# Conditioning the first half of the channels first, and row and column groups for the samples' small products

## The chip, the core and the metric

The kernel runs on one core of one Trainium2 chip. The metric is the device time of one execution in microseconds (us), less is better. The engines are TensorE (PE, the matmuls; its weight loads are shown apart as PEld), VectorE (DVE), ScalarE (ACT), GpSimd (POOL) and SyncE (SP, which issues most of the transfers). Each engine works through its own instructions in the order of the program, and waits at the head of that row for what its next instruction needs.

## The reference, cut to what matters

One layer for 1024 prompt tokens and 8 requests of 8 sample tokens (64 columns more, 1088 in all), 1024 channels, fp32:

```
mod = silu(c) @ w_ada + b_ada
sh1, sc1, g1, sh2, sc2, g2 = split(mod, 6)          # 1024 each
h = rms_norm(x, norm_mix_pre) * (1 + sc1) + sh1
proj = h @ w_in                                     # z, xbc, dt, qkv, gate, beta, alpha
# SSD: 16 heads x 64, state (64, 128) per head;  GDN: 8 heads, state (128, 128) per head
# for a sample request b (8 tokens) the state that comes in is state_ssd[b], state_gdn[b]:
y_off  = C @ h_in * exp(acs)                        # SSD: product with the old state
h_last = h_in * exp(acs_end) + B^T @ (x dt decay)   # SSD: the state's update
v_new  = U - W @ S ;  o = q_in @ S + attn @ v_new   # GDN: products with the old state
S_last = S * g_end + k_out^T @ v_new                # GDN: the state's update
x = x + g1 * rms_norm(concat(y, o) @ w_out)
x = x + g2 * rms_norm(swiglu(modulated rms_norm(x)))
```

The prompt's requests start from a state of zeros, the samples' 8 requests each from a state of their own. All new states are outputs.

## The kernel before

**Large products.** A weight tile is split in a high part (`wh`, cast on ACT, L161) and the rest (`wl`, subtracted on DVE, L162), the activations likewise (`hh`, `hl`), and a product is three matmuls (L186 to L188 in `gemm`, L1262 to L1265 for w_out). The 1088 columns go in thirds, `TH` = 384, 384 and 320. Of the weights, `load_tile` brings 128 columns in two halves of 0.26 MB.

**Order.** PE's row of instructions is that in which the code is written (`manual_schedule` of PE); the scheduler orders the other engines. Smaller work is written as generators, started with `spawn`. `gemm` calls `tick()` after k = 2, 5 and 7, and each tick lets every generator go on to its next `yield`. So the SSD pairs (`ssd_pair`) and the samples' GDN (`gdn_samples`) stand between the large products, as does `hidden_rest`, which makes the second and third thirds of the hidden columns.

**The beginning.** `ada_block(cb)` loads 512 columns of w_ada (2 MB) and multiplies (L255): the 1024 rows are taken 128 at a time, and k modulo 4 picks 32 of the PE's columns, so four products go to four groups of 32 output partitions. `ada_cols` folds the four groups and turns the result into channels on partitions (L281), into `modT` (shift: blocks 0 and 1; scale: blocks 2 and 3). The blocks come in the order 0, 1, 2, 3, with the loads of x tiles 0 to 2 between them on SP, then come the weights of K and Q and x3 to x8. `norm_x` (ACT L246, DVE L118 and L248) scales x rows, `turned` transposes (L307), and `modulated` gives `hh` (ACT L338), `ht` (DVE L340) and `hl` (DVE or POOL L349). For the first third all eight k are made, and then the gemms of K and Q run.

**SSD samples.** A pair of heads handles 128 state rows. For each half a (4 requests) the old state is transposed to `h0T` (a tile `hS`, three buffers, ACT copy L1047), and 4 matmuls of 128x128 weights with 8 columns each give the product with C (L1063). At the end L1077 is the last use of the decay tile `L`, of which there are two, and then the state is updated in two matmuls with 64 rows of weights and 512 columns (L1084, one per half, with a yield between). `decays` (L976 to L983) makes the next pair's `L`: a load, nine subtractions on DVE per head, an exponential on ACT; L995 multiplies it by `cb`, and L1044 uses it.

**GDN samples.** Per head and request one matmul of 128x128 weights and 128 columns, eight summed in one bank (L1436): the weights `kb` hold the request's k and q in 8 columns of its own each and zeros elsewhere. L1444, L1454 follow, then the update in two matmuls of 64 rows and 512 columns (L1461), with a yield behind each.

Of the kernel before, what the change touches and what calls it, by code (L numbers as in the profile page):

```python
# [8 lines left out]
F32 = mybir.dt.float32  # L9
# [7 lines left out]
P = 128  # L17
D = 1024
KD = D // P
NP = 1024  # L20
# [23 lines left out]
def hybrid_step(ctx: ExitStack, tc: tile.TileContext, x_p, x_s, c_p, c_s, st_ssd, st_ssdc, st_gdn, st_gdnc,  # L44
# [60 lines left out]
    sel = const.tile([P, 9], F32, name="sel")  # L105
    dve.tensor_tensor(out=sel, in0=fold[:, 0:9], in1=ident[:, 9:10].to_broadcast([P, 9]), op=ALU.add)
# [111 lines left out]
    cc = gk.tile([P, NP], F32, name="gate")[0:9]  # L218
    act.dma_start(out=cc[0:1, :], in_=c_p)
    act.dma_start(out=cc[1:9, :], in_=c_s)  # L220
    act.activation(out=cc, in_=cc, func=AF.Silu)
    pool.memset(caF, 0.0)
    ps = bank()
    pcv = ps[:, 0:KD * 9].rearrange("p (k n) -> p k n", n=9)
    for k in range(KD):
        pe.transpose(pcv[:, k, :], cc[:, k * P:(k + 1) * P], ident[0:9, 0:9])
    dve.tensor_copy(caF[:, :, 0:9], pcv)
# [7 lines left out]
    def load_x(i):  # L235
# [4 lines left out]
        sp.dma_start(out=xt[0:n], in_=x_p[i * P:(i + 1) * P, :] if i < NC else x_s)  # L240
# [8 lines left out]


# [6 lines left out]
    bias = [init.tile([P, 512], F32, name=f"bias{i}") for i in range(2)]  # L257
    for t in bias:
        pool.memset(t, 0.0)

    def ada_block(cb, between):
        ps = ps_a.tile([P, 512], F32, name="ps")
        act.dma_start(out=bias[cb % 2][9:10, :], in_=b_ada[:, cb * 512:(cb + 1) * 512])
        for k in range(0, KD, 2):
# [4 lines left out]
            if k == 2:  # L269
                between()  # L270
            if cb == 3 and k == 4:
                turn.extend(turned(0, i) for i in range(2))
        rows = init.tile([P, 512], F32, name="rows", bufs=2)
        dve.tensor_tensor(out=rows, in0=ps, in1=bias[cb % 2], op=ALU.add)
        return rows

    def ada_cols(cb, rows):
        ps = bank()
        pv = ps[:, 0:4 * 9].rearrange("p (k n) -> p k n", n=9)
        for i in range(4):  # L280
            pe.matmul(pv[:, i, :], lhsT=rows[:, i * P:(i + 1) * P], rhs=sel, start=True, stop=True)  # L281
        dve.tensor_copy(modT[:, cb // 2, 4 * (cb % 2):4 * (cb % 2) + 4, :], pv)
# [4 lines left out]
    act.dma_start(out=r1[0:8, :], in_=n_mix_pre[0].rearrange("(r c) -> r c", c=P))  # L287
    act.dma_start(out=r1[8:16, :], in_=n_ffn_pre[0].rearrange("(r c) -> r c", c=P))
    act.dma_start(out=r1[16:24, :], in_=ssd_nw[0].rearrange("(r c) -> r c", c=P))
    act.dma_start(out=r1[24:25, :], in_=gdn_nw)  # L290
    act.dma_start(out=r1[25:37, :], in_=ssd_cb[0].rearrange("(r c) -> r c", c=P))
    act.dma_start(out=r1[37:85, :], in_=ssd_cw[0].rearrange("j (r c) -> (j r) c", c=P))
    act.dma_start(out=r2, in_=gdn_cw[0].rearrange("j (r c) -> (j r) c", c=P))
    def params():
        ps = bank()
# [14 lines left out]
    turn = []  # L310
    rows = ada_block(0, params)
# [5 lines left out]
    for i in (3, 4, 5):  # L317
        load_x(i)
    first.append(load_tile(w_in, C_Q))
    for i in (6, 7, 8):  # L320
        load_x(i)
    ada_cols(3, rows)
    W_MIX, W_FFN, W_SSDN, W_GDNN = (prm1T[:, a:b] for a, b in ((0, 8), (8, 16), (16, 24), (24, 25)))
# [10 lines left out]
    def modulated(ps, k, c0, n, hi, lo, pool_, low=dve):  # L334
# [7 lines left out]
        if m < n:  # L342
# [8 lines left out]
    dve.scalar_tensor_tensor(out=modT[:, 1], in0=modT[:, 1], scalar=1.0,  # L351
                             in1=W_MIX.unsqueeze(2).to_broadcast([P, KD, 9]), op0=ALU.add, op1=ALU.mult)

    hid_box = {}

    def hidden(g, step):
        c0, n = TH[g]
        for k in range(KD):
# [32 lines left out]
    for _ in hidden(0, KD):  # L391
        pass
# [1441 lines left out]
```

## Time and profile before

| | us |
|---|---|
| median of 3 runs | 2081.65 (2078.68 to 2083.41) |
| the profiled execution | 2084.96 |
| its span in the profile | 2083.2 |
| PE busy | 2003.6 (96%) |
| DVE busy | 1380.3 (66%) |
| ACT busy | 940.1 (45%) |
| POOL busy | 240.9 (12%) |

A row of a timeline gives the start, the time that the instruction took, the engine, the line, the operation with output and inputs, the tile's rows and columns for PE, and how many instructions of the same kind follow one another. Behind them in brackets stands how long the engine was idle before, and what ended that. Starts on PE are measured and ends modelled, so distances are taken from start to start. A plain fp32 matmul shows as two records (x8 are four matmuls).

### The profile page before, as it was taken

The page shows a single profiled execution, that of the slowest core. Times are in us where ns is not written, and L with a number is a line of the kernel's source. Part 1 is how long each engine was busy: PE and PEld are TensorE (multiplying, and loading weights), DVE is VectorE, ACT ScalarE, POOL GpSimd, SP SyncE. Part 2 cuts the span into 40 slices and gives each one's busy share as a digit, 9 for nine tenths or more (in the row PEclk, how much of TensorE's full clock was granted, in tenths as well). Part 3 has the DMA queues.
Part 4 walks back from the last instruction along what each step waited for, and adds up shares of the span by engine and source line. Part 5 has one row for each costly group of instructions (what it writes and reads, how often), then busy time and mean ns, then how long its engine had stood idle before and what let it go on. Part 6 is the DMA issues. An engine that isn't in the chain of part 4 may idle for free. (4 is left out here: it accounts for less than half of the span.)

```text
span 2083.2 us, 35078 instructions
## 1 busy us (share of the span) xinstructions
PE 2003.6 (96%) x13075; PEld 1783.9 (86%) x13075; DVE 1380.3 (66%) x3071; ACT 940.1 (45%) x2241; POOL 240.9 (12%) x238
## 2 busy tenths in 40 slices
PE   6999999999999999899999999999999999999998
PEld 3888999999999988788867667899999999988886
DVE  3769787788778548657647758895555556745465
ACT  3545545554544443334423447663333334544354
POOL 2211010011100023323213210000000000000000
PEclk9999999999999999999999999999999999999999
DMA  9122121121111266465466757532222223643131
GB/s 295 29 69 55 38 63 52 51 64 50 53 56 57 75 203 196 141 207 185 151 214 199 233 157 223 153 91 78 78 79 78 79 73 107 226 141 107 46 100 48
DMA packets 224763, 239.45 MB, mean 115 GB/s; under 512 B 19141, under 2 KB 177391, under 8 KB 224464
## 3 DMA queue, kind: packets, MB, share of 16 engines
q1 hardware_dynamic: 218320, 232.33, 36.0%
q10 hardware_dynamic: 5952, 3.75, 0.6%
q8 instruction: 103, 1.69, 0.3%
q0 software_dynamic: 320, 1.12, 0.2%
q14 instruction: 68, 0.56, 0.1%
HBM read 190.92 MB, written 46.25 MB: 114 GB/s over the span
## 5 line engine op out<-in xcount | busy, mean ns | idle before, releaser
L186 PE MATMUL ps<-hh,wh 128*128 128x384 f32 (+1 forms) x1248 | 445.4, 357 | 1.5 <-ACT sz L566 1.5
L187 PE MATMUL ps<-hl,wh 128*128 128x384 f32 (+1 forms) x1248 | 412.4, 330 | 2.8 <-DVE hl L349 1.6
L188 PE MATMUL ps<-hh,wl 128*128 128x384 f32 (+1 forms) x1248 | 411.2, 329 | 0.0
L1262 PE MATMUL ps<-wh,sh 128*128 128x512 f32 x678 | 277.7, 410 | 3.3 <-ACT wh L161 2.5
L1265 PE MATMUL ps<-wl,sh 128*128 128x512 f32 x678 | 270.8, 399 | 3.6 <-DVE wl L162 3.5
L186 PEld LDWEIGHTS ps<-hh,wh 128*128 128x128 f32 x1248 | 238.7, 191 | 25.4 <-issue 19.8
L187 PEld LDWEIGHTS ps<-hl,wh 128*128 128x128 f32 x1248 | 238.8, 191 | 5.8 <-DVE hl L349 2.6
L1264 PE MATMUL ps<-wh,sl 128*128 128x512 f32 x604 | 241.0, 399 | 2.0 <-DVE sl L1275 2.0
L188 PEld LDWEIGHTS ps<-hh,wl 128*128 128x128 f32 x1248 | 237.5, 190 | 0.0
L161 ACT CAST wh<-wr 128x512 fp32r<-128x512 f32 x200 | 123.3, 622 | 214.8 <-PE ps L187 103.3
L1262 PEld LDWEIGHTS ps<-wh,sh 128*128 128x128 f32 x678 | 128.8, 190 | 50.4 <-issue 16.4
L162 DVE TENSOR_TENSOR wl<-wd,wh 128x512 fp32r<-128x512 f32 x130 | 89.6, 692 | 122.8 <-ACT wh L161 122.5
L162 DVE TENSOR_TENSOR wl<-wr,wh 128x512 fp32r<-128x512 f32 x174 | 123.5, 714 | 56.2 <-ACT wh L161 55.3
L1265 PEld LDWEIGHTS ps<-wl,sh 128*128 128x128 f32 x678 | 128.7, 190 | 36.8 <-DVE wl L162 6.1
L161 ACT CAST wh<-wd 128x512 fp32r<-128x512 f32 x130 | 80.7, 621 | 143.5 <-PE ps L1264 103.2
L1264 PEld LDWEIGHTS ps<-wh,sl 128*128 128x128 f32 x604 | 115.1, 191 | 26.6 <-DVE sl L1275 2.3
L1320 POOL TENSOR_TENSOR r<-r,mhalf 128x1 f32<-128x1 f32 (+1 forms) x18 | 12.8, 719 | 821.8 <-DVE r L1318 818.9
L1735 PE MATMUL ps<-T_0h,wh 128*128 128x272 f32 x352 | 103.6, 294 | 3.1 <-DVE u L1751 1.8
L1737 PE MATMUL ps<-T_0h,wl 128*128 128x272 f32 x352 | 102.7, 292 | 0.7 <-DVE wl L1673 0.7
L1735 PE MATMUL ps<-T_1h,wh 128*128 128x272 f32 x352 | 102.2, 290 | 0.5 <-ACT as L1742 0.5
L1736 PE MATMUL ps<-T_0l,wh 128*128 128x272 f32 x352 | 102.1, 290 | 0.0
L1737 PE MATMUL ps<-T_1h,wl 128*128 128x272 f32 x352 | 101.9, 289 | 0.0
(473 smaller groups left out, 4528.1 us busy)
## 6 DMA issues: line engine op xcount, KB each, us to landing
wr<-in_w_in_dram SPq DMA_DIRECT2D x104, 256.0 KB
wr<-in_w_gate_up_dram SPq DMA_DIRECT2D x104, 256.0 KB
wr<-in_w_out_dram SPq DMA_DIRECT2D x96, 256.0 KB
w<-in_w_ada_dram SPq DMA_DIRECT2D x16, 1024.0 KB
wd<-in_w_down_dram SPq DMA_DIRECT2D x22, 512.0 KB
actdr<-as SPq DMA_DIRECT2D x18, 544.0 KB
L<-accr SPq DMA_DIRECT2D x16, 544.0 KB
am<-actdr SPq DMA_DIRECT2D x44, 192.0 KB
```

The lines of the kernel that those rows point to most:

```text
L161: act.copy(wh, src)
L162: low.tensor_tensor(out=wl, in0=src, in1=wh.bitcast(F32), op=ALU.subtract)
L186: pe.matmul(out, lhsT=hi[k], rhs=xh[k], start=(k == 0), stop=False)
L187: pe.matmul(out, lhsT=hi[k], rhs=xl[k], start=False, stop=False)
L188: pe.matmul(out, lhsT=lo[k], rhs=xh[k], start=False, stop=(k == KD - 1))
L1262: pe.matmul(o, lhsT=sh[:, cs], rhs=wh, start=first, stop=False)
L1264: pe.matmul(o, lhsT=sl[:, cs], rhs=wh, start=False, stop=False)
L1265: pe.matmul(o, lhsT=sh[:, cs], rhs=wl, start=False, stop=last)
L1320: pool.tensor_tensor(out=r[0:n, 0:1], in0=r[0:n, 0:1], in1=mhalf[0:n], op=ALU.pow)
L1735: pe.matmul(o, lhsT=wh[:, cs], rhs=bh[:, m, :], start=(m == 0 and not on), stop=False, **on)
L1736: pe.matmul(o, lhsT=wh[:, cs], rhs=bl[:, m, :], start=False, stop=False, **on)
L1737: pe.matmul(o, lhsT=wl[:, cs], rhs=bh[:, m, :], start=False, stop=(m == 3), **on)
```

## The change

**The beginning.** Blocks 0 and 2 (shift and scale of channels 0 to 511) come first, then the first weight halves of K and Q; `first_half(0)` makes the hidden k 0 to 3 of the first third and writes their 24 matmuls. Then come blocks 1 and 3, the second halves, the loads of x3 to x8, and `first_half(1)` with the rest, a tick behind each k of each product. x0 to x2 load through ACT's queue. The four biases come in one transfer, norm_mix_pre as a tenth row of the tile that is transposed for the conditioning, and the other small parameters load later.

**SSD samples.** C^T is copied once a group of heads into a padded tile `cz` (32 columns around each request's 8). The product with the old state is done once a pair: eight matmuls with 32 columns of weights and 128 columns of the old state, in four column groups and two rounds. Its result has tokens on partitions, so it is copied by ACT (`yo`) and transposed. The update takes 32 rows for each half, in two row groups, one bank each, back to back.

**GDN samples.** The eight matmuls become sixteen with 32 columns of weights, in four column groups; the update takes two row groups back to back, with two yields behind it.

The core of the diff:

```diff
-    def ada_block(cb, between):
-        ps = ps_a.tile([P, 512], F32, name="ps")
+    def ada_block(cb, between=None):
+        ps = bank()
...
-    for cb in range(1, 4):
-        load_x(cb - 1)
-        norm_x(cb - 1)
-        rows = ada_block(cb, lambda: ada_cols(cb - 1, rows))
-    first = [load_tile(w_in, C_K)]
...
+    def first_half(h):
+        for _ in hidden(0, KD, range(4 * h, 4 * h + 4)):
+            pass
+        t0, n = TH[0]
+        for (hi, lo), o in zip(first, first_ps):
+            for k in range(4 * h, 4 * h + 4):
+                xh, xl = hh[k][:, t0:t0 + n], hl[k][:, t0:t0 + n]
+                pe.matmul(o, lhsT=hi[k], rhs=xh, start=(k == 0), stop=False)
+                pe.matmul(o, lhsT=hi[k], rhs=xl, start=False, stop=False)
+                pe.matmul(o, lhsT=lo[k], rhs=xh, start=False, stop=(k == KD - 1))
+                if h:
+                    tick()
+
+    rows = ada_block(0)
+    for i in range(3):
+        norm_x(i)
+    rows2 = ada_block(2, lambda: ada_cols(0, rows))
+    for load in loads:
+        load(0)
+    ada_cols(2, rows2)
+    first_half(0)
+    rows = ada_block(1)
+    rows2 = ada_block(3, lambda: ada_cols(1, rows))
+    for load in loads:
+        load(1)
+    ada_cols(3, rows2)
+    for i in range(3, NT):
+        load_x(i)
...
-    neacs = cA.tile([P, NT, 24], F32, name="neacs")
+    neacs = cA.tile([P, NT, HG], F32, name="neacs")
...
-            pos = bank()
-            for i in range(4):
-                b = (4 * a + i) * TS
-                pe.matmul(pos[:, i * TS:(i + 1) * TS], lhsT=h0T[:, i, :], rhs=cT[:, NP + b:NP + b + TS], start=True,
-                          stop=True)
+            if a == 1:
+
+                pos = bank()
+                for r in range(2):
+                    for i in range(4):
+                        pe.matmul(pos[32 * i:32 * i + 32, 0:P], lhsT=cz[:, i, 24 * r:24 * r + 32], rhs=h0Ts[r][:, i, :],
+                                  start=r == 0, stop=r == 1)
+                yo = sd.tile([P, 4, P], F32, name="hS", bufs=3)[:, 0, :]
+                act.copy(yo, pos[:, 0:P])
...
+        pe.transpose(ps[:, P:2 * P], yo, ident)
...
-        for a in range(2):
-            ps = bank()
-            pe.matmul(ps, lhsT=xe[0:NS, NC].rearrange("p h n -> p (h n)"),
-                      rhs=bb[:, 4 * a:4 * a + 4, :].rearrange("p b n -> p (b n)"), start=True, stop=True)
+        pss = [bank() for _ in range(2)]
+        for a, ps in enumerate(pss):
+            r = slice(32 * a, 32 * a + 32)
+            pe.matmul(ps, lhsT=xe[r, NC].rearrange("p h n -> p (h n)"),
+                      rhs=bb[r, 4 * a:4 * a + 4, :].rearrange("p b n -> p (b n)"), start=True, stop=True)
...
-            for b in range(NB):
-                pe.matmul(pk[:, 0:P], lhsT=kb[:, P * b:P * b + P], rhs=S0[:, b, :], start=(b == 0),
-                          stop=(b == NB - 1))
+            for i in range(4):
+                for q in (0, 2, 1, 3):
+                    b = 4 * (q % 2) + i
+                    pe.matmul(pk[32 * q:32 * q + 32, 0:P], lhsT=kb[:, P * b + 32 * q:P * b + 32 * q + 32],
+                              rhs=S0[:, b, :], start=(i == 0), stop=(i == 3))
...
-            for a in range(2):
-                ps = bank()
-                pe.matmul(ps, lhsT=ko[:, h, :], rhs=ub[:, 4 * a:4 * a + 4, :].rearrange("p b n -> p (b n)"),
+            pss = [bank() for _ in range(2)]
+            for a, ps in enumerate(pss):
+                r = slice(32 * a, 32 * a + 32)
+                pe.matmul(ps, lhsT=ko[r, h, :], rhs=ub[r, 4 * a:4 * a + 4, :].rearrange("p b n -> p (b n)"),
                           start=True, stop=True)
```

Three places show how the instructions stand. Lines of the changed kernel have numbers of their own: L268 is the ada product (L255 before), L287 its turning (L281), L320 the transposes of x (L307), L408 to L410 the first third's matmuls, L189 to L191 gemm's (L186 to L188). In these listings xN counts instructions.

PE at the beginning, before: ada products, their turning, transposes of x, and gemm.

```order
L281 MATMUL ps<-sel,rows 128x9 x4
L255 MATMUL ps<-w_295,caF 32x512 x2
L307 MATMUL ps<-ident,kq 128x128 x6
L255 MATMUL ps<-w_307,caF 32x512 x2
L281 MATMUL ps<-sel,rows 128x9 x4
L307 MATMUL ps<-ident,kq 128x128 x18
L186 MATMUL ps<-hh_124,wh 128x384
```

The same place in the changed kernel; in the place of the line of dots stand the other matmuls of k 0 to 3, 24 in all.

```order
L268 MATMUL ps<-w_240,caF 32x512 x2
L287 MATMUL ps<-sels,rows 128x9 x4
L320 MATMUL ps<-ident,kq 128x128 x12
L408 MATMUL ps<-hh_127,wh 128x384
L409 MATMUL ps<-hl_135,wh 128x384
...
L410 MATMUL ps<-hh_130,wl 128x384
L268 MATMUL ps<-w_321,caF 32x512 x2
L268 MATMUL ps<-w_325,caF 32x512 x2
```

Behind the second of four blocks PE now goes on to transposes and 24 matmuls, and the ada products of the third block stand behind these.

ACT there, before (L161 casts weights, L338 is hh, L246 the sum of squares of a norm; kq, w are x tiles):

```order
L246 ACTIVATE jk,ss<-kq 128x1024 x2
L161 CAST wh<-wr 128x512 x2
L338 ACTIVATE hh_124<-ps,modT 128x384
L338 ACTIVATE hh_125<-ps,modT 128x384
L338 ACTIVATE hh_126<-ps,modT 128x384
```

ACT there in the changed kernel, for k 4 to 7 (L164, L338 and L252 are the same three):

```order
L164 CAST wh<-wr 128x512 x2
L252 ACTIVATE jk,ss<-kq 128x1024
L338 ACTIVATE hh_131<-ps,modT 128x384
L338 ACTIVATE hh_132<-ps,modT 128x384
L338 ACTIVATE hh_133<-ps,modT 128x384
L338 ACTIVATE hh_134<-ps,modT 128x384
L252 ACTIVATE jk,ss<-w_383 128x1024
```

The norm of x3 stands ahead of hh of k 4 to 7, and before it stood behind all eight.

PE in the second half and the end of the first SSD pair, before (L1053 are the prompt's products with the state, L1070 a transpose):

```order
L1053 MATMUL ps<-cT,hS 128x128 x4
L1063 MATMUL ps<-cT,hS 128x8 x4
L186 MATMUL ps<-hh_127,wh 128x384
...
L188 MATMUL ps<-hh_129,wl 128x384
L1070 MATMUL ps<-ident,hS 128x128
L1077 MATMUL ps<-L,xd 64x64 x2
L1084 MATMUL ps<-bb,xe 128x512
L186 MATMUL ps<-hh_130,wh 128x384
...
L188 MATMUL ps<-hh_131,wl 128x384
L1084 MATMUL ps<-bb,xe 128x512
```

The same in the changed kernel (L1103, L1122 and L1133 are L1053, L1070 and L1077):

```order
L1103 MATMUL ps<-cT,hS 128x128 x4
L1115 MATMUL ps<-hS,halT 32x128 x8
L189 MATMUL ps<-hh_130,wh 128x384
...
L191 MATMUL ps<-hh_132,wl 128x384
L1122 MATMUL ps<-ident,hS 128x128
L1123 MATMUL ps<-ident,hS 128x128
L1133 MATMUL ps<-L,xd 64x64 x2
L1141 MATMUL ps<-bb,xe 128x512 x2
L189 MATMUL ps<-hh_133,wh 128x384
```

The eight 32-column products L1115 stand in the second half alone, a transpose L1123 follows nine gemm matmuls later, and both updates L1141 stand together.

## Rows read from the trace of the kernel before

**Rows 1.** The page, first part: busy time, share of the span, instructions.

```profile
PE 2003.6 (96%) x13075; PEld 1783.9 (86%) x13075; DVE 1380.3 (66%) x3071; ACT 940.1 (45%) x2241; POOL 240.9 (12%) x238
```

**Rows 2.** Windows, beginning: busy of PE, PEld, DVE, ACT, POOL; PEclk, DMA share, GB/s.

```profile
20.00:30.00 10.00, 7.02 (x34) 1.75 (x28) 3.10 (x8) 2.70 (x5) 0.76 (x2) 0.98 1.04 367
```

**Rows 3.** Timeline, PE, the beginning: start, us, instruction, idle time before.

```profile
35.70 1.05 PE L255 MATMUL ps<-w,caF 128*32 128x512 f32 x4
...
41.84 0.42 PE L186 MATMUL ps<-hh,wh 128*128 128x384 f32 x1
...
56.99 0.34 PE L188 MATMUL ps<-hh,wl 128*128 128x384 f32 x1
...
64.61 0.44 PE L186 MATMUL ps<-hh,wh 128*128 128x384 f32 x1
```

**Rows 4.** Timeline, ACT, the beginning.

```profile
39.20 4.61 ACT L338 ACTIVATE hh<-ps,modT 128x384 fp32r<-128x384 f32 x8 [3.01 <-DVE modT L351]
43.66 1.09 ACT L246 ACTIVATE jk<-kq 128x1024 bf16<-128x1024 f32 x1
```

**Rows 5.** Timeline, DVE, the beginning.

```profile
40.23 1.26 DVE L340 TENSOR_SCALAR ht<-ps,modT 128x384 f32<-128x384 f32 x2
...
48.46 0.67 DVE L340 TENSOR_SCALAR ht<-ps,modT 128x384 f32<-128x384 f32 x1
...
50.80 0.76 DVE L248 TENSOR_SCALAR kq<-kq,rs 128x1024 f32<-128x1024 f32 x1 [1.50 <-POOL rs L119]
...
58.45 1.26 DVE L340 TENSOR_SCALAR ht<-ps,modT 128x384 f32<-128x384 f32 x2 [1.21 <-ACT hh L338]
```

**Rows 6.** Timeline, PE, the second half of the first SSD pair.

```profile
785.92 1.06 PE L255 MATMUL ps<-w,caF 128*32 128x512 f32 x8
786.91 0.45 PE L186 MATMUL ps<-hh,wh 128*128 128x384 f32 x1
787.19 0.34 PE L187 MATMUL ps<-hl,wh 128*128 128x384 f32 x1
...
788.59 1.05 PE L1053 MATMUL ps<-cT,hS 128*128 128x128 f32 x8
789.48 0.96 PE L1063 MATMUL ps<-cT,hS 128*128 128x8 f32 x8
790.29 0.42 PE L186 MATMUL ps<-hh,wh 128*128 128x384 f32 x1
...
791.94 0.27 PE L1070 MATMUL ps<-ident,hS 128*128 128x128 f32 x1
...
792.40 1.12 PE L1084 MATMUL ps<-bb,xe 64*128 64x512 f32 x2
```

**Rows 7.** Waits at L1044: PE's idle time before it, releaser, us and times.

```profile
  DVE L L995: 13.2, 11
```

**Rows 8.** Timeline, PE, products of 32 rows and 32 columns in GDN's prompt.

```profile
184.91 0.21 PE L814 MATMUL ps<-qs,rc 32*32 32x32 f32 x1
184.94 0.19 PE L812 MATMUL ps<-rc,qs 32*32 32x32 f32 x1
```

**Rows 9.** Timeline, PE, one head of GDN's samples among w_out's matmuls.

```profile
1119.51 1.95 PE L1436 MATMUL ps<-s_S,s_kqb 128*128 128x128 f32 x16
1121.21 0.48 PE L1262 MATMUL ps<-wh,sh 128*128 128x512 f32 x1
...
1125.26 0.66 PE L1444 MATMUL ps<-s_Y,s_R 64*64 64x128 f32 x2 [2.39 <-DVE s_kqb L1432]
...
1132.06 1.12 PE L1461 MATMUL ps<-s_ub,s_ko 64*128 64x512 f32 x2
1133.11 0.50 PE L1262 MATMUL ps<-wh,sh 128*128 128x512 f32 x1
```

**Rows 10.** Timeline, SP, the load of the next pair's L.

```profile
792.49 0.82 SPq L976 DMA_DIRECT2D L<-accr  x2
```

**Rows 11.** Timeline, ACT, the copy of the second half's old state.

```profile
786.08 0.59 ACT L1047 COPY hS<-ps 128x512 f32<-128x512 f32 x1 [1.91 <-PE ps L622]
```

More of the change, by code (lines that the diff above doesn't have):

```diff
@@ L239, in load_x @@
         xt = xts[i]
[L240 removed]
+        q.dma_start(out=xt[0:n], in_=x_p[i * P:(i + 1) * P, :] if i < NC else x_s)
     def norm_x(i):
@@ L248, in norm_x @@
         dve.tensor_scalar(out=xt[0:n], in0=xt[0:n], scalar1=rs[0:n, i:i + 1], scalar2=None, op0=ALU.mult)
+    for i in range(3):
+        load_x(i, act)
+    for k in range(KD):
+        pe.transpose(pcv[:, k, :], cc[:, k * P:(k + 1) * P], ident[0:10, 0:10])
+    dve.tensor_copy(caF[:, :, 0:9], pcv[:, :, 0:9])
+    dve.tensor_copy(wmix, pcv[:, :, 9])
     def ada_rows(ps, w, ks):
@@ L268, in ada_block @@
             ada_rows(ps, lambda k: w2[:, k % 2, :], (k, k + 1))
-            if k == 2:
+            if k == 2 and between:
                 between()
-            if cb == 3 and k == 4:
-                turn.extend(turned(0, i) for i in range(2))
         rows = init.tile([P, 512], F32, name="rows", bufs=2)
-        dve.tensor_tensor(out=rows, in0=ps, in1=bias[cb % 2], op=ALU.add)
+        dve.tensor_tensor(out=rows, in0=ps, in1=bias, op=ALU.add)
         return rows
@@ L308, in turned @@
         return ps
[L310 to L323 removed]
+    W_FFN, W_SSDN, W_GDNN = (prm1T[:, a:b] for a, b in ((8, 16), (16, 24), (24, 25)))
     def ssd_tap(i, j):
@@ L349, in modulated, with hidden @@
         low.tensor_tensor(out=lo[:, 0:n], in0=ht[:, 0:n], in1=hi[:, 0:n].bitcast(F32), op=ALU.subtract)
-    dve.scalar_tensor_tensor(out=modT[:, 1], in0=modT[:, 1], scalar=1.0,
-                             in1=W_MIX.unsqueeze(2).to_broadcast([P, KD, 9]), op0=ALU.add, op1=ALU.mult)
     hid_box = {}
-    def hidden(g, step):
+    def hidden(g, step, ks=range(KD)):
         c0, n = TH[g]
-        for k in range(KD):
-            ps = turn.pop(0) if turn else turned(g, k)
+        for k in ks:
+            ps = turned(g, k)
             modulated(ps, k, c0, n, hh[k][:, c0:c0 + n], hl[k][:, c0:c0 + n], init,
@@ L379, in halos, with hidden_rest, tile_halves, load @@
         hid_box["halos"] = clock[0]
+    def hidden_rest():
+        for i in range(3, NT):
+            norm_x(i)
+        yield from wait(5)
+        yield from hidden(1, 3)
+        yield from hidden(2, 3)
+    def tile_halves(c0):
+        hi, lo = [], []
+        def load(half):
+            wh, wl = load_half(w_in[512 * half:512 * half + 512, c0:c0 + P].rearrange("(k p) m -> p k m", p=P))
+            for k in range(4):
+                hi.append(wh[:, k * P:(k + 1) * P])
+                lo.append(wl[:, k * P:(k + 1) * P])
+        return (hi, lo), load
+    first, loads = zip(*(tile_halves(c) for c in (C_K, C_Q)))
+    first_ps = [ps_a.tile([P, 512], F32, name="ps")[:, 0:TH[0][1]] for _ in first]
+    def first_half(h):
[11 more added lines that the diff above has]
+    rows = ada_block(0)
+    for i in range(3):
+        norm_x(i)
+    rows2 = ada_block(2, lambda: ada_cols(0, rows))
[8 more added lines that the diff above has]
+    ada_cols(3, rows2)
+    for i in range(3, NT):
+        load_x(i)
     wsr = gk.tile([P, 4, NS], F32, name="sm").rearrange("p a t -> p (a t)").rearrange("p (k m) -> p k m", m=32)
@@ L389, in hybrid_step @@
     dve.tensor_sub(wst[:, :, 32:64], wsr, wst[:, :, 0:32].bitcast(F32))
-    for _ in hidden(0, KD):
-        pass
-    def hidden_rest():
-        for i in range(3, NT):
-            norm_x(i)
-        yield from wait(5)
-        yield from hidden(1, 3)
-        yield from hidden(2, 3)
+    spawn(params())
+    spawn(later(halos(), 4))
     spawn(hidden_rest())
-    spawn(later(halos(), 4))
+    first_half(1)
     dcol = cA.tile([P, KD], F32, name="dcol")
@@ L846, in first_two @@
         raws = [conv_raw() for _ in wts]
-        for g in range(3):
+        for ps, raw in zip(first_ps, raws):
+            raw[2](ps, *TH[0], TH[0][1])
+        for g in range(1, 3):
             for wt, raw in zip(wts, raws):
```

84 lines of the change are left out of this document (51 added, 33 removed).

## The prediction

> **What bounds the kernel now.** First the page's line of busy times: TensorE (PE) works 2003.6 us, 96% of the span, and no other engine more than 66% [rows 1]. So what the change takes out of PE's row of instructions counts almost in full, unless PE then waits for something that was ready just in time. Second, the stretches in which PE is not full. At the beginning it is fed by transfers, at 367 GB/s between 20 and 30 us [rows 2], and then by VectorE (DVE) and ScalarE (ACT), which normalise and modulate x [rows 4, 5]. In the SSD pairs its L1044 waits for the decays L, 13.2 us in 11 waits [rows 7]. Third, the small products themselves, read as the distance from the start of one to the start of what follows on PE [rows 6, 9], since ends on PE are modelled.
>
> **The beginning.** Before, the last ada product starts at 35.70, the first gemm at 41.84, the last matmul of the first third of K and Q at 56.99, and the second third at 64.61 [rows 3]. Between 41.84 and 56.99, 15.2 us, stand 48 matmuls; eight undisturbed ones take 1.40 us (787.19 to 788.59) [rows 6], 48 would take 8.4. The rest is ACT's hh (8 in 4.61 us) and DVE's ht and hl behind the last modT [rows 4, 5]. The change lets half of this, k 0 to 3 and 24 matmuls, run while blocks 1 and 3 arrive. Step by step:
> - Ahead of the last ada weights now lie two more weight halves of 0.26 MB: 0.52 MB at 0.367 MB/us [rows 2] = 1.4 us. The last ada product moves from 35.70 to 37.1. From there to hh it took 3.5 us (39.20 [rows 4]), so 40.6.
> - In ACT's new order the norm of x3 stands ahead of hh of k 4, and DVE's scaling of x3 ahead of ht. x3 comes behind two more halves and is 0.52 MB itself: 1.05 MB, 2.9 us, after the ada weights. With ACT's 1.09 us [rows 4] and DVE's 0.76 [rows 5] ht starts at about 43 instead of 40.23.
> - Then four k instead of eight. Eight took from 40.23 to 49.1 [rows 5], 1.1 us each, so four end at 47.4, and the low half on GpSimd about 48.3. K's last three matmuls and Q's twelve follow, 2.6 us: Q ends at 50.9 against 57.2, 6.2 us earlier.
> - The next step must move as well. DVE begins hidden(1) at 58.45 [rows 5], behind the norms of x3 to x8. Five norms are left behind k 7: on ACT at 1.09 they end about 50, on DVE at 0.76 and the small steps between them about 52, so hidden(1) starts near 52.5, 6 us earlier, and the second third with it.
>
> I take **6 us**, from 2 (x3 to x8, now last on the queue, land late and hold hh) to 10 (x3's norm holds nothing).
>
> **SSD samples, 8 pairs.** The products with the old state took 0.81 us a half (789.48 to 790.29), 1.62 a pair [rows 6]. Now they are eight matmuls of 32 columns in four column groups, two rounds of 128. The trace has four column groups at work together: the four matmuls L255 of 512 columns go by in 0.99 us (785.92 to 786.91) [rows 6], and a single plain fp32 matmul of 512 columns needs 1.05 (1132.06 to 1133.11) [rows 9]. Two rounds of 128 are half of that, 0.5; the added transpose takes up to 0.27, as L1070 [rows 6], and I put 0.2. Saved: 0.9 a pair. The state update L1084, at 792.40 [rows 6], has the shape of the one at 1132.06, twice 1.05. The yield between its halves costs one change of shape: the first gemm matmul behind a small stretch lasts 0.28 (786.91 to 787.19) instead of 0.17, so 0.1. As two row groups side by side it is 1.05 once, 1.15 saved. That different tiles run together is seen where L812 and L814 start 0.03 us apart and out of their order [rows 8]; that two do which share all 128 columns no row shows. So this term lies between 0.1 (one after the other) and 1.15, and I take 1.15: two tiles that share no cell, with outputs in two banks, are nearest to that row. Together 2.05 x 8 = 16.4 us.
>
> Less of it stays. The update lies between L1077, which frees L, and the next pair's L1044, which waits for L; L's load issues at 792.49, just behind L1077 [rows 10], and its way through DVE and ACT is left as it was. Eleven waits, two to a pair [rows 7], are five or six of the seven intervals: there the 1.15 turns into waiting, -5.8. The products with the state lie ahead of L1077, and what they save stays.
>
> Then the new waits. The old-state copies share three buffers hS, and both must now live until the common product. So ACT's second copy waits for the first product with the state before it (L1053, 788.59 [rows 6]) instead of starting at 786.08 [rows 11], and round 2 needs it three L1053 and one round later: 0.59 us of copy and two signals against 0.67 + 0.25. Held behind it on ACT for up to 2.5 us are raw evacuations and weight casts wh; gemm needs these a third later, which hides them, and ACT had stood idle 1.91 us [rows 11]. Without that cover PE would wait for a bank. I put 0.2 a pair, 1.6, between 0 and 6.4 (the whole copy and its signals, 0.8). DVE's one multiplication for two and ACT's extra copy of the result lie beside the nine gemm matmuls ahead of the transpose. 16.4 - 5.8 - 1.6 = 9.0; because ACT and DVE pace this stretch for the exponentials too I keep **7 us**, from 2 (all intervals lose the update, the copy is bare) to 13 (three intervals lose it, the copy is hidden).
>
> **GDN samples, 8 heads.** Eight full matmuls took 1.70 us (1119.51 to 1121.21) [rows 9]. Sixteen of 32 columns are four rounds of 128, a quarter of 0.99 each: 1.0; their 32 records at 0.03 us [rows 8] come to the same. So 1.0 to 1.15, and 0.6 is saved. The update is 1.05 twice [rows 9] and one change of shape less: 1.15, or 0.1 in series. 1.75 x 8 = 14. w_out's matmuls fill PE here, but in one head PE waited 2.39 us for DVE's work on the head [rows 9], and such a wait grows by what is saved ahead of it. I keep about 80%: **11.5 us**, from 4 to 14. The shorter neacs and the biases' single transfer lie off PE and count nothing.
>
> The sum against the profiled execution (2084.96, 1.8 of it around the span): 2084.96 - 24.5 = 2060.5. It was 3.3 above the median of the runs, 2081.65, so the median goes to **2057**.
>
> Two rules of the Trainium skill bear on this. TensorEngine Tiling (Array Packing), Key Properties, says that a change of tiling mode drains the engine; by the trace that is the 0.1 us behind a small stretch, no more. TensorE: Matmul & The Clock Gate, Part 3, says that a weight load overlaps running matmuls only where its row group differs; the new column-group products all use every row, so by it each pays for its load (third rival).
>
> **The rivals.**
> 1. Row groups that share columns run in series: no row shows otherwise. Then the GDN updates lose 8.4, 6.9 of it at the rate kept, and in SSD the pairs whose update counted lose 2.6: gain 15, **2067**.
> 2. The beginning and the SSD pairs give theirs back: x3's norm ahead of hh costs what the early half won, and the held copy makes exponentials and casts late. For it: DVE and ACT pace the beginning [rows 4, 5], and L is late already [rows 7]. Against it: ACT's idle time ahead of the copy [rows 11]. Only GDN stays, **2070**.
> 3. Column groups pay one after another for their weights. Each small matmul then costs what a full one does, 1.70 / 8 = 0.21 [rows 9]: sixteen take 3.4 a head, 1.7 x 8 = 13.7 more, and SSD's products about 2 more. The beginning (6), GDN's updates (7.4) and SSD's (3.4) gain 16.8, the copy costs 1.6: about **2081**, no change. Against it: L255, whose four matmuls each bring their own weights [rows 6]. This is what the page's rule on loads would do.
> 4. Slower: no two groups overlap, rows or columns, because a product of 128 columns is over before the next has its weights. Then 13.7 + 2 + 1.6 stand against 6 + 0.9: **2092**. With the updates in series it turns to a loss where the sixteen take more than 2.1 us a head. Against it: L255, though that has 512 columns, and L812, with 32 [rows 6, 8].
>
> **How the numbers follow.** Forecast 0.65 (2048 to 2063); rival 1 0.14; rival 2 0.09; rival 3 0.05; rival 4 0.07. The range's low end, 2045, is all terms at their upper ends (10 + 13 + 14 = 37); its high end, 2072, takes in rivals 1 and 2 and leaves out 3 and 4. About 0.2%, 4.2 us, is what a measurement of this kernel tells from no change. Faster: 0.65 + 0.14 + 0.09 = 0.88; the same 0.05; slower 0.07.
>
> **What would show it.** In the profile after: the second third's first gemm at 58 to 60 us; 0.5 us for SSD's sample products and 1.05 for each update, to the next gemm; 1.0 to 1.15 for GDN's product. Waits for L that are longer by about 1 us a pair show the update lost there; idle time of PE ahead of round 2, ended by ACT's copy, shows the held copy. A GDN product of 1.7 or more, updates of 2.1, or a second third later than 62 would each prove its term wrong.

## The result and the profile after

| | median, us | ratio to the kernel before, 95% interval |
|---|---|---|
| before, 8 executions | 2080.25 (2077.02 to 2084.84) | |
| changed, 8 executions | 2071.77 (2055.52 to 2074.15) | 0.9945 (0.992 to 0.9971) |
| changed, timed once more (e5) | 2064.9 (2062.31 to 2072.66) | 0.9933 (0.9908 to 0.9958) |

The change makes the kernel faster by 0.55%, 11 us, and by 0.67%, 14 us, when timed again. Forecast were 24.5 us, a time of 2057. The time lies just inside the range (2045 to 2072); of the forecast gain the first timing has less than half, the second little more than half. The profiled execution took 2074.15 us, its span 2072.4; it is the slowest of the eight.

What the page says of PE after (first part: busy time, share, instructions), against [rows 1]:

```profile
PE 1982.2 (96%) x13211; PEld 1779.0 (86%) x13211; DVE 1381.5 (67%) x3066; ACT 944.9 (46%) x2255; POOL 229.4 (11%) x239
```

PE is busy for 21 us less, and still 96% of the span. The small products did what was forecast. The timeline of PE after, in the first SSD pair (against [rows 6]) and in one head of GDN's samples (against [rows 9]):

```profile
792.74 0.65 PE L1115 MATMUL ps<-hS,halT 128*32 128x128 f32 x16
793.31 0.44 PE L189 MATMUL ps<-hh,wh 128*128 128x384 f32 x1
...
795.12 0.27 PE L1123 MATMUL ps<-ident,hS 128*128 128x128 f32 x1
795.32 0.33 PE L1133 MATMUL ps<-L,xd 64*64 64x64 f32 x4
795.58 1.13 PE L1141 MATMUL ps<-bb,xe 32*128 32x512 f32 x4
796.64 0.44 PE L189 MATMUL ps<-hh,wh 128*128 128x384 f32 x1
...
1127.81 1.08 PE L1496 MATMUL ps<-s_S,s_kqb 128*32 128x128 f32 x32
1128.82 0.50 PE L1319 MATMUL ps<-wh,sh 128*128 128x512 f32 x1
...
1135.66 1.13 PE L1523 MATMUL ps<-s_ub,s_ko 32*128 32x512 f32 x4
1136.72 0.50 PE L1319 MATMUL ps<-wh,sh 128*128 128x512 f32 x1
```

From start to start: the eight 32-column products 0.57 us (forecast 0.5), their transpose 0.20, the two updates together 1.06 (1.05), GDN's sixteen 1.01 (1.0 to 1.15), its updates 1.06. So row groups that share all columns do run side by side, and column groups do not pay one after another for their weights: rivals 1, 3 and 4 are out. The waits of PE do not follow. Waits of PE before and after (what waited, for what: us in total, times, longest):

```profile
PE ps L1044 <- DVE L L995: 7.3, 6, 2.6
...
PE ps L255 <- DMA w<-in_w_ada_dram: 5.5, 3, 2.6
...
PE ps L1264 <- DVE sl L1275: 2.0, 1, 2.0
...
PE ps L186 <- ACT sz L566: 1.5, 2, 1.3
```

```profile
PE ps L1093 <- DVE L L1043: 7.0, 5, 2.0
PE ps L1321 <- DVE sl L1332: 6.4, 2, 3.9
PE ps L268 <- DMA w<-in_w_ada_dram: 5.3, 3, 3.9
...
PE ps L1072 <- POOL xe L1055: 4.1, 3, 2.0
...
PE ps L189 <- ACT sz L606: 3.0, 1, 3.0
```

The waits for L are what they were. Beside them stands a new one, for xe, 4.1 us, which PE did not wait for before, and two have grown: for sl (the low part of what w_out multiplies) from 2.0 to 6.4 us, and for sz from 1.5 to 3.0. The waits for sl lie behind the SSD pairs, at 1056 and 1103 us. They come with the products in column groups: 6.4 us in each profile with the whole SSD part (e2, e4, e5, e13), 1.5 to 2.0 in those without its products (e1, e3, e9, e10, e12). What a wait can cost beyond itself is seen behind it. PE after, 835 to 845 us:

```profile
835.89 1.16 PE L1072 MATMUL ps<-xe,btk 128*128 128x128 f32 x8 [1.56 <-POOL xe L1055]
837.13 0.47 PE L1093 MATMUL ps<-L,xd 128*64 128x128 f32 x2
839.10 1.97 PE L1093 MATMUL ps<-L,xd 128*64 128x128 f32 x14 [1.49 <-DVE L L1043]
...
842.23 0.52 PE L190 MATMUL ps<-hl,wh 128*128 128x384 f32 x1
842.55 0.52 PE L191 MATMUL ps<-hh,wl 128*128 128x384 f32 x1
...
844.34 0.34 PE L191 MATMUL ps<-hh,wl 128*128 128x384 f32 x1
844.52 0.72 PE L1103 MATMUL ps<-cT,hS 128*128 128x128 f32 x5
```

Behind the two waits gemm's matmuls start 0.32 us apart (842.23 to 842.55), 1.2 GHz, and 0.18 from 844.34 on, 2.4 GHz. Not every wait is followed by that: in e14 below PE waits five times in the SSD pairs, for 1.56 to 2.15 us, and the granted clock stays at 1.00. The same shows as a mean over the stretch between the first and the last product with xe. Windows over it of before, then after, then the changed kernel once more (e5; length, busy of PE, PEld, DVE, ACT, POOL; mean granted clock PEclk, DMA share, GB/s):

```profile
776.70:1037.20 260.50, 249.37 (x1719) 212.11 (x1718) 175.05 (x407) 99.50 (x168) 79.06 (x51) 0.98 0.57 178
```

```profile
780.70:1044.40 263.70, 244.45 (x1717) 209.13 (x1716) 176.68 (x398) 103.77 (x178) 76.60 (x52) 0.94 0.57 175
```

```profile
771.20:1031.10 259.90, 239.96 (x1717) 205.56 (x1716) 176.21 (x398) 103.69 (x178) 76.62 (x52) 0.96 0.58 178
```

From before to after the stretch became 3.2 us longer. Split it in three: PE idle (length less busy), 11.1 and 19.3; loss by the clock (length times what PEclk lacks to 1), 5.2 and 15.8; the rest, 244.2 and 228.6, is work at 2.4 GHz. The work fell by 15.6 us, the forecast's 16.4. Idle time took 8.2 of it and the clock 10.6. (The clock counts while PE waits too, so where waits are long this loss is an upper value. PEclk has two digits, so the loss is good to 1.3 us.)

One execution of each is not enough for the length: in e5 the changed kernel's stretch is 0.6 us shorter than before's. The five profiles with the SSD part as before (before, e1, e3, e9, e12) have 257.3 to 262.9 us, mean 260.3; the four with the whole change of it (changed, e2, e4, e5) 259.9 to 265.0, mean 262.8. The parts move alike in all of them: from the five to the four the mean work falls by 16.1 us, idle time grows by 9.3 and the loss by the clock by 9.3. So the saved work is gone in waits and clock, and the stretch did not become shorter; that it became longer is not shown.

### The profile page after: what moved, and what is told of

It reads as the page before. It is cut to its first block, busy times and chain, and to the rows that moved or that the text cites. A ratio compares the mean times of both kernels' runs of the same rounds, so it can differ in the third digit from the quotient of the medians.

```text
span 2072.4 us, 35364 instructions
## 1 busy us (share of the span) xinstructions
PE 1982.2 (96%) x13211; PEld 1779.0 (86%) x13211; DVE 1381.5 (67%) x3066; ACT 944.9 (46%) x2255; POOL 229.4 (11%) x239
## 5 line engine op out<-in xcount | busy, mean ns | idle before, releaser
L189 PE MATMUL ps<-hh,wh 128*128 128x384 f32 (+1 forms) x1232 | 442.5, 359 | 3.2 <-ACT sz L606 3.0
L191 PE MATMUL ps<-hh,wl 128*128 128x384 f32 (+1 forms) x1232 | 408.3, 331 | 0.0
L189 PEld LDWEIGHTS ps<-hh,wh 128*128 128x128 f32 x1232 | 236.6, 192 | 26.4 <-issue 19.1
L191 PEld LDWEIGHTS ps<-hh,wl 128*128 128x128 f32 x1232 | 235.5, 191 | 0.0
L164 ACT CAST wh<-wr 128x512 fp32r<-128x512 f32 x200 | 123.4, 621 | 211.8 <-PE ps L190 114.7
L1319 PEld LDWEIGHTS ps<-wh,sh 128*128 128x128 f32 x678 | 128.8, 190 | 41.9 <-issue 12.5
L165 DVE TENSOR_TENSOR wl<-wr,wh 128x512 fp32r<-128x512 f32 x174 | 120.7, 696 | 52.9 <-ACT wh L164 50.6
L164 ACT CAST wh<-wd 128x512 fp32r<-128x512 f32 x130 | 80.7, 621 | 138.1 <-PE ps L1321 99.5
L1737 DVE TENSOR_TENSOR wl<-wr,wh 128x512 fp32r<-128x512 f32 x78 | 53.7, 691 | 71.7 <-ACT wh L1736 70.3
```

Source lines behind the costliest of these rows:

```text
L164: act.copy(wh, src)
L165: low.tensor_tensor(out=wl, in0=src, in1=wh.bitcast(F32), op=ALU.subtract)
L189: pe.matmul(out, lhsT=hi[k], rhs=xh[k], start=(k == 0), stop=False)
L191: pe.matmul(out, lhsT=lo[k], rhs=xh[k], start=False, stop=(k == KD - 1))
L1319: pe.matmul(o, lhsT=sh[:, cs], rhs=wh, start=first, stop=False)
L1737: dve.tensor_tensor(out=wl, in0=opa[p], in1=wh.bitcast(F32), op=ALU.subtract)
```

## The experiments

All ratios are to the kernel before, timed in the same set. The SSD stretch is that between the first and the last product with xe, of the one profiled execution, split as above.

| run | ratio (95% interval) | stretch | idle | clock | work |
|---|---|---|---|---|---|
| before | 1 | 260.5 | 11.1 | 5.2 | 244.2 |
| changed | 0.9945 (0.992 to 0.9971) | 263.7 | 19.3 | 15.8 | 228.6 |
| e5 changed, once more | 0.9933 (0.9908 to 0.9958) | 259.9 | 19.9 | 10.4 | 229.6 |
| e1 beginning alone | 0.9977 (0.9957 to 0.9997) | 261.8 | 10.0 | 7.9 | 243.9 |
| e2 SSD samples alone | 1.0036 (1.0015 to 1.0056) | 262.7 | 20.1 | 15.8 | 226.8 |
| e3 GDN samples alone | 0.9946 (0.9927 to 0.9965) | 258.9 | 11.1 | 2.6 | 245.2 |
| e4 changed, gap filled | 0.99 (0.9875 to 0.9925) | 265.0 | 20.4 | 15.9 | 228.7 |
| e6 e4, SSD waits filled | 0.9962 (0.9946 to 0.9978) | 268.1 | 11.7 | 8.0 | 248.4 |
| e7 before, short way to L | 0.995 (0.9929 to 0.997) | 249.3 | 3.5 | 2.5 | 243.3 |
| e8 e2, short way to L | 0.9906 (0.9883 to 0.993) | 239.9 | 7.4 | 4.8 | 227.7 |
| e9 changed, SSD undone | 0.9914 (0.9891 to 0.9936) | 257.3 | 9.4 | 2.6 | 245.3 |
| e10 e9 and updates | 0.9928 (0.9908 to 0.9948) | 262.2 | 16.9 | 10.5 | 234.8 |
| e11 e9 and products | 1.0016 (0.9999 to 1.0034) | 283.6 | 33.6 | 19.9 | 230.1 |
| e12 e9, gap filled | 0.9907 (0.9886 to 0.9929) | 262.9 | 11.2 | 7.9 | 243.8 |
| e13 changed, xd first | 0.9901 (0.9879 to 0.9923) | 257.6 | 18.3 | 10.3 | 229.0 |
| e14 e11, h first | 0.987 (0.985 to 0.9889) | 250.9 | 11.7 | 0.0 | 239.2 |
| e15 e14, xd first | 0.9888 (0.9867 to 0.9909) | 253.0 | 11.7 | 2.5 | 238.8 |

**Each part alone (e1, e2, e3).** The kernel before with one part of the diff each: everything up to `first_two` with `neacs` (e1), `ssd_group` and `ssd_pair` (e2), `gdn_samples` (e3).

> The kernel before with the change's beginning alone; samples as before. Reading of the two traces (theory A): the second third starts at 66.5 us instead of 64.6 because PE is granted half its clock from 46.7 us on, and by 112 us the changed kernel is 1.5 us behind, so this run is 0 to 3 us slower than before (2080 to 2083), with the half clock between 45 and 70 us in its trace. The prediction's sum (theory B): 6 us faster, 2074.

> The kernel before with the SSD samples' change alone. Theory A (PE's 11 us of saved work in this stretch are turned into waits for L, xe and the weights): 0 to 4 us slower than before, 2080 to 2084, with PE idle before the L products longer by about 8 us in all. Theory B (prediction): 7 us faster, 2073.

> The kernel before with the GDN samples' change alone. Theory A: the whole gain of the changed kernel is here, 12 to 15 us, 2065 to 2068. Theory B (prediction): 11.5 us, 2069. If neither and the gain is under 6, the other two parts help more than the traces say.

Measured: 0.23% faster (4.8 us), 0.36% slower (7.5), 0.54% faster (11.3). The sum, 0.41%, is near the whole change. GDN has nearly all of the gain, the beginning most of its forecast 6, against my reading of the two traces (theory A of e1), and the SSD part has the wrong sign, with a loss beyond theory A's 0 to 4 us. The changed kernel's first profile had met one of the slower beginnings: the first product of the rates (L479, L519 after) starts between 106.8 and 113.4 us in nine executions with the new beginning and unfilled gaps, mean 109.9, and between 107.6 and 123.4 in five with the old one, mean 114.6. In the three with filled gaps (e4, e6, e12) it starts between 106.4 and 107.8.

**The changed kernel again (e5).**

> The changed kernel itself once more, beside the next three on the same chip. It should come out 8 to 12 us under the kernel before, as in its first timing; a difference of more than 5 us from that would say that the beginning's clock changes from one set of executions to the next.

It was 0.67% faster than before, 14 us, against the 8 to 12 expected; the first timing's interval overlaps.

**The gap at the beginning filled (e4, and e12 without the SSD part).** In `first_half(1)`, whose results nobody reads:

```diff
+                if k == 4 and o is first_ps[0]:
+                    fill(6)
                 pe.matmul(o, lhsT=hi[k], rhs=xh, start=(k == 0), stop=False)
+                if k == 4 and o is first_ps[0]:
+                    fill(14)
                 pe.matmul(o, lhsT=hi[k], rhs=xl, start=False, stop=False)
```

> The changed kernel with 20 more matmuls of 384 columns, whose results nobody reads, around the first matmul of k 4 of K, where PE waits for hl (3.5 us of work in a gap of about 3.5). Clock theory: PE keeps the full granted clock from 47 to 69 us, the second third starts at 60 to 62 instead of 66.5, and the run is 4 to 6 us faster than the changed kernel's 2072, 2066 to 2068. Rival (ACT's and DVE's norms set the second third): the clock may be full but the third starts at 65 or later and the time stays 2071 to 2075.

> e9 with the 20 unread matmuls of e4 in the beginning's gap. If those keep the clock (e4 was 9 us under the changed kernel's first timing), 2 to 6 us faster than e9. If e4's lead came from the spread of the beginning alone, equal to e9 within 2 us.

e4 looked like a proof: 1.0% under before and the second third at 61.4 us. e12 takes it back: with and without the filling 0.9907 and 0.9914, the second third at 60.8 and 61.4. Between 45 and 50 us the filling does hold the granted clock, windows of e9 and then of e12:

```profile
45.00:50.00 5.00, 4.91 (x24) 3.78 (x22) 2.99 (x8) 3.51 (x7) 3.28 (x5) 0.66 1.06 227
50.00:55.00 5.00, 3.76 (x20) 3.39 (x19) 3.84 (x10) 2.90 (x5) 1.17 (x3) 0.73 0.13 34
```

```profile
45.00:50.00 5.00, 4.92 (x30) 3.71 (x28) 3.00 (x8) 3.53 (x8) 3.28 (x5) 1.00 0.87 193
50.00:55.00 5.00, 3.82 (x21) 3.32 (x21) 3.79 (x10) 2.86 (x5) 1.21 (x3) 0.67 0.12 30
```

But DVE, ACT and GpSimd do the same in both, and they set what PE does next; the clock falls a little later anyway. So the clock's share at the beginning is not shown to cost time. e4's lead over the changed kernel stays open, since their intervals overlap; beginnings differ by several us from one execution to the next.

**A shorter way to L (e7, e8).** In `decays`, in the kernel before and in e2:

```diff
-            for c in range(NT):
-                w = slice(c * P, min(c * P + P, T))
-                dve.tensor_scalar(out=t[:, w], in0=t[:, w], scalar1=acs[:, c, h:h + 1], scalar2=0.0,
-                                  op0=ALU.subtract, op1=ALU.min)
```

> The kernel before with a shorter way to L: the nine subtractions on DVE per head are left out (L is only loaded and exponentiated, its numbers are wrong by that), 4.7 us of DVE work less per pair between the load and the exponential. PE's waits for L before L1044 should fall from 13 us to under 4 and the half clock behind them go: 8 to 20 us faster than before.

> e2 (the SSD samples' change alone) with the same subtractions left out. Theory (the saved work is on PE, and the late L turns it into waits and half clock): it is 8 to 16 us faster than e7, where e2 was 7 us slower than before. Rival (the SSD change itself adds waits, as the held copy and the transpose): it is again no faster than e7.

e7 is 0.5% and e8 0.94% faster than before: with L early, and DVE freed of 18 subtractions a pair, the SSD part that cost 7.5 us gains about 9 (0.44% between the two, 11 between their medians). In the stretch, work falls by 15.6 us from e7 to e8 and the length by 9.4. The saving is real: where the subtractions are left out, it counts.

**The waits filled (e6).** Four unread matmuls ahead of the products with xe, four and six around the first L product, in all pairs but the first:

```diff
+            if j and a == 0:
+                dummy(pst[:, 0:384], 4)
...
+                    if j and a == 0 and i == 0:
+                        dummy(py[:, P:512], (4, 6)[hd])
```

> The kernel of e4 with 14 more unread matmuls of 384 columns in each SSD pair but the first: 4 ahead of the products with xe, 4 ahead of the L products and 6 between their first two, 98 in all, 17 us of PE work at the full clock. Clock theory (each wait of 2 us and more is followed by 4 to 6 us at half the clock, 17 to 19 us lost between 750 and 1050 us): the loss by the clock there falls under 8 us, PE's idle time there falls by 12 or more, and the run is 2 to 8 us faster than e4 (2061.7 against 2083.3) although it computes more. Rival (the half clock costs nothing there, since PE waits for L anyway): the 17 us of work fill the waits and what does not fit is paid: the run is 0 to 6 us slower than e4.

e6 is 0.62% behind e4, 13 us, more than the rival's 0 to 6, and 6 us behind the changed kernel timed in the same set (e5). Against e4, idle time in the stretch fell by 8.7 us (12 or more were expected) and the loss by the clock by 7.9, and the stretch became 3.1 longer, since 19.7 us of work were added. So the clock recovers when PE is kept busy, but what keeps it busy costs at least as much; where the other 10 us are lost is open.

**The SSD part in pieces (e9, e10, e11).** e9 undoes `ssd_group` and `ssd_pair` of the change; e10 adds the updates in row groups to that, e11 the products in column groups.

> The changed kernel with the SSD samples' part undone (beginning and GDN samples changed). Theory (the SSD part costs 5 us, since its saved PE work turns into waits for L and the half clock behind them): 16 us faster than before, some 4 us faster than e5. Rival (the SSD part is neutral and e2 met bad beginnings): equal to e5, 12 us faster than before.

> e9 with the SSD state's update in two row groups, the products with the old state as before. Theory: the 1.15 us a pair lie between the last use of L and the next L product, so they all become waiting: 0 to 4 us slower than e9 (the half clock). Rival: they count, 5 to 9 us faster than e9.

> e9 with the SSD samples' product with the old state in column groups, the update as before. Theory: these 0.9 us a pair lie between L's first use and its release, inside the loop that sets the pair's period, so they count: 3 to 7 us faster than e9. Rival (any PE work saved in this stretch turns to waits and half clock): 0 to 3 us slower than e9.

e9 is 0.86% faster than before, so the change is at least as fast without its SSD part. The updates (e10) come as the theory had it: against e9 10.5 us less work, 7.5 more idle, 7.9 more by the clock, the stretch 4.9 longer. e9's stretch is the shortest of the five with the same SSD part; against their mean, 260.3, e10's is 1.9 longer, and the intervals of the two times overlap. So the saved work brings nothing; that it costs is not shown by this pair. The products (e11) turned both expectations over: the time is 20 us above e9's. Waits of PE in e11 (what waited, for what: us in total, times, longest):

```profile
PE ps L662 <- DMA h<-in_state_ssd_dram: 21.1, 4, 7.6
...
PE ps L1072 <- POOL xe L1055: 4.3, 3, 2.0
```

That is a wait no one had named: for the next pair's old state h. The timeline of e11's DVE between the first two pairs shows why, and then its SP:

```profile
791.67 0.68 DVE L1142 TENSOR_TENSOR h<-ps,h 128x512 f32<-128x512 f32 x1
792.27 1.28 DVE L1152 TENSOR_TENSOR y<-y,sz 128x1088 f32<-128x1088 f32 x1
794.28 3.56 DVE L1027 TENSOR_SCALAR L<-L,rate 128x128 f32<-128x128 f32 x18 [0.73 <-DMA L<-accr]
797.75 0.68 DVE L1142 TENSOR_TENSOR h<-ps,h 128x512 f32<-128x512 f32 x1
798.35 0.68 DVE L1054 TENSOR_TENSOR xd<-ps,dt 128x512 f32<-128x512 f32 x1
```

```profile
798.46 0.39 SPq L1146 DMA_DIRECT2D out_dram<-h  x1
...
801.79 0.40 SPq L1041 DMA_DIRECT2D h<-in_state_ssd_dram  x1
```

The second addition to the state (L1142) stands behind the 18 subtractions of L, and even behind the wait for L's load. Only then the state is stored, at 798.46, and the next state is loaded into the same tile, at 801.79; PE's transposes of it waited until 812.05. L itself was not late: its subtractions begin 19.3 us behind the first product with xe, as in the changed kernel. The scheduler, which orders DVE, had put the addition there when the program around it changed. In the changed kernel both additions come ahead, but both halves of xd, from which GpSimd makes xe, stand behind the subtractions, where before had one half ahead. DVE's order between the first two pairs, before and changed:

```
L1086 TENSOR_TENSOR h_8756<-ps,h_8756 128x512
L1006 TENSOR_TENSOR xd<-ps,dt 128x512
L979 TENSOR_SCALAR L<-L,rate_422 128x128 x8

L1027 TENSOR_SCALAR L<-L,rate_643 128x128 x8
L1027 TENSOR_SCALAR L<-L,rate_643 128x64
L1054 TENSOR_TENSOR xd<-ps,dt 128x512 x2
```

**The order put right (e13, e14, e15).** The same instructions with a priority; e13 marks xd and xe in the changed kernel, e14 the additions to h in e11, e15 both in e11:

```diff
+            with tc.high_priority(PRIO):
                 dve.tensor_tensor(out=xd[:, c4], in0=pv, in1=dts[:, c4].to_broadcast([P, 4, 2, 64]), op=ALU.mult)
                 pool.tensor_tensor(out=xe[:, c4], in0=xd[:, c4], in1=dec[:, c4].to_broadcast([P, 4, 2, 64]), op=ALU.mult)
...
+            with tc.high_priority(PRIO):
                 dve.tensor_tensor(out=h0[:, 4 * a:4 * a + 4, :], in0=ps.rearrange("p (b n) -> p b n", n=P),
                                   in1=h0[:, 4 * a:4 * a + 4, :], op=ALU.add)
```

> The changed kernel with DVE's two multiplications to xd and GpSimd's to xe raised in the scheduler's priority, so that on DVE they stand ahead of the 18 subtractions of L as they mostly did before the change. Theory (the SSD part costs because it turns this order round: xe is late and L times cb runs beside xe, 1.95 us each instead of 1.24): PE's waits for xe vanish, the SSD stretch from its first to its last xe product falls from 260 to 264 to under 257 us, and the run is 16 to 22 us faster than before. Rival (L's own way sets the pair whatever the order): within 2 us of e5's distance of 17 or the first timing's 11.

> e11 with DVE's additions to the sample state h raised in priority, so that the second stands ahead of the subtractions of L. Theory (in e11 it stood behind them, the state left late, and the next state's load, which reuses its tile, kept PE waiting 7.4, 2.9, 3.3 and 7.6 us): those waits vanish and the run is 12 to 20 us faster than e11, that is 10 to 17 us faster than before. Rival (something else in the column-group products costs): it stays within 5 us of e11.

> e14 with xd and xe raised as well, as in e13. Theory: the products' 0.9 us a pair now count, 3 to 7 us faster than e9, 20 to 25 us faster than before. Rival: the saved work becomes waiting for L all the same, equal to e9 (17 to 18 us faster than before).

e14 moves e11's ratio from 1.0016 to 0.987: two additions a pair that stand elsewhere are worth about 30 us (0.0146 of 2080), more than the 12 to 20 expected. It is the fastest kernel of the study, 1.3% (27 us) under before, and its interval lies under both timings of the changed kernel. Its waits of PE for the state are gone. Windows of e9 and then e14 over the stretch:

```profile
777.50:1034.80 257.30, 247.88 (x1719) 211.04 (x1719) 176.50 (x407) 99.57 (x168) 78.91 (x51) 0.99 0.58 180
```

```profile
782.00:1032.90 250.90, 239.16 (x1718) 198.80 (x1718) 179.19 (x399) 103.72 (x178) 76.18 (x52) 1.00 0.59 184
```

The products alone, in a good order, take 6.1 us of work away and shorten the stretch by 6.4 (9.4 against the mean of the five). e9 did not run with the priority, so the order's part in this is not split off. xd first removes the waits for xe in e13, but those for L grow to 12.1 us in nine waits (7.0 in five in the changed kernel). Its ratio, 0.9901, is under the changed kernel's, with intervals that overlap; the time, 21 us under before, is in the theory's range, and the stretch missed its 257 by 0.6. On top of e14 the same priority (e15) brings nothing, within the intervals. e13 against e15 is the update once more, with both orders good: 9.8 us less work, 6.6 more idle and 7.8 more by the clock, the stretch 4.6 longer.

e14 tells the update from DVE's order. Timelines of DVE between the first two pairs, of the changed kernel and then of e14:

```profile
797.35 1.28 DVE L1144 TENSOR_TENSOR h<-ps,h 128x512 f32<-128x512 f32 x2
...
799.98 4.66 DVE L1027 TENSOR_SCALAR L<-L,rate 128x128 f32<-128x128 f32 x18
804.56 1.28 DVE L1054 TENSOR_TENSOR xd<-ps,dt 128x512 f32<-128x512 f32 x2
```

```profile
800.47 0.68 DVE L1143 TENSOR_TENSOR h<-ps,h 128x512 f32<-128x512 f32 x1
801.23 4.66 DVE L1027 TENSOR_SCALAR L<-L,rate 128x128 f32<-128x128 f32 x18
805.81 1.27 DVE L1054 TENSOR_TENSOR xd<-ps,dt 128x512 f32<-128x512 f32 x2
```

Both have the additions ahead of the subtractions and all of xd behind them, here and between all the other pairs. So xd's place alone is not what costs: the fastest kernel has it too. Besides the priority, e14 and the changed kernel differ in the update alone, and without the two row groups the stretch is 250.9 us instead of 259.9 to 265.0 (the four profiles above) and the ratio 0.987 instead of 0.9945 and 0.9933, 13 to 16 us. With the products in column groups, then, the updates save 10 to 11 us of work and lose more than that. They also stand back to back; no run tells this from the row groups.

## Why the prediction was right and wrong

- **What the small products cost**: right. All four measured as forecast, and the work at 2.4 GHz in the SSD stretch fell by 15.6 us of 16.4 (16.1 in the means). The unseen price, row groups that share columns, was the upper one taken, 1.06 us for both.
- **GDN samples**: right, 11.3 us (e3) of 11.5.
- **The beginning**: the size agrees, 4.8 us (e1; interval 1 to 9) of 6, but the steps do not, so the agreement is in good part luck. Rows of the changed kernel's timeline, of ACT, DVE and PE:

```profile
43.27 2.34 ACT L338 ACTIVATE hh<-ps,modT 128x384 fp32r<-128x384 f32 x4
...
44.88 1.26 DVE L340 TENSOR_SCALAR ht<-ps,modT 128x384 f32<-128x384 f32 x2
...
56.29 1.26 DVE L340 TENSOR_SCALAR ht<-ps,modT 128x384 f32<-128x384 f32 x2
...
61.06 0.52 PE L410 MATMUL ps<-hh,wl 128*128 128x384 f32 x1
...
66.50 0.69 PE L189 MATMUL ps<-hh,wh 128*128 128x384 f32 x1
```

  hh of k 4 starts at 43.27 instead of 40.6, ht at 44.88 instead of 43 (the terms shown for it, 37.1 + 2.9 + 1.09 + 0.76, come to 41.9), Q's last matmul at 61.06 where Q was to end at 50.9, hidden(1) on DVE at 56.29 instead of 52.5, and the second third at 66.5, later than before's 64.61 [rows 3] and than the 62 that was to prove the term wrong. What was left out is that the norms of x4 to x8 share ACT's queue with the evacuation of K, and PE's row of instructions between Q's last k takes up transposes that wait for those norms. The size came out near because the old beginning is often slow (the product of the rates at 107.6 to 123.4 us, mean 114.6), and before's profiled one was a good one, 111.6.
- **SSD samples**: wrong, 7 us of gain forecast and 7.5 of loss measured (e2; interval 3 to 12), 4 to 6 by e9 against the two timings of the changed kernel. The step that failed is "16.4 - 5.8 - 1.6 = 9.0": it takes 7.4 us off for waits and nothing for the clock. In the means of the profiles 16.1 us of work went, idle time took 9.3, the clock took 9.3 more, and nothing of the gain is left in the stretch. Behind it the waits for sl add 4.4 us, which no term had. Four things were missing in the step.
  1. No price for the clock. It was put at nothing, and is the larger part of what the step lacks: idle time alone is not far from the 7.4 taken off. The sign that was named, longer waits for L, shows in e10 (11.8 us in ten waits) and not in the changed kernel (7.0 in five), where PE waits for other things.
  2. The update was to keep 3.4 of its 9.2 us. It keeps nothing: the stretch is not shorter with it beside the old products (e10) and longer beside the new ones (4.6 us in e13 against e15, one profile each, and 9 to 14 in the changed kernel against e14, where the times agree).
  3. The other engines' order was taken as left as it was. The scheduler made a new one for DVE: xd behind the subtractions in the changed kernel, the state's addition behind them in e11. The addition's place decides whether the products bring 6 us (e14) or cost 20 (e11); xd's place gains nothing in e15 and perhaps some us in e13. It could have been read before the run: the same order listing that showed ACT's queue shows DVE's.
  4. [rows 7] was misread. 13.2 us in 11 waits counts PE's loads and matmuls each for itself; PE's matmuls waited 7.3 us in 6 waits, two in each of three pairs, not five or six. Read rightly it would have taken less off, and put the forecast still higher.
- **The held copy** was priced at 1.6 us and cost nothing seen: PE waits ahead of no round 2; once 0.2 us for yo's copy, ahead of its transpose.
- **Rivals.** The second, with 2070, came nearest in number, but not by its mechanism: the beginning did not give its gain back (e1), and the SSD part lost its own by idle time and clock, not by the held copy. The terms of the third give a loss of 0.5 us, 2082, not 2081. The page of the Trainium skill on which the third rested, TensorE: Matmul & The Clock Gate, Part 3, says that loads overlap only across row groups; sixteen column-group products in 1.01 us show overlap here without that.

What stays open: whether the updates lose by their row groups or by standing back to back, what makes sl late, and why e4 was so fast.

## What to carry to other kernels

Before PE work is counted as saved, ask what PE waits for next and whether the saved instructions stand inside the loop that frees that thing or behind it; what stands behind it turns into waiting, and waiting can be followed by matmuls at half the clock, so that it can cost as much as the work did or more. After every change of a hand-ordered engine read what the scheduler made of the others' order, and look for a short instruction that a buffer's store and reload hangs on behind a long run; one addition out of place cost more here (e11, about 30 us) than all the packing of that stage could gain. And profile the same kernel more than once before a few us in a stretch are explained.

## What the runs showed of the hardware

Row groups of 32 that share all 128 columns run side by side, with outputs in two banks: two products of 512 columns in 1.06 us, where one of 64 rows took 1.05. Sixteen 32-column products of 128 columns in four column groups go by in 1.01 us. And the spread of one kernel's time goes along with its mean granted clock: in the eight executions of the changed kernel from 0.985 at 2055.52 us to 0.978 at 2074.15.
